# Output projection in two passes over tokens, with the FFN's input norm under the second pass

## The chip, the cores and the metric

The kernel runs as one program on the eight cores of one Trainium2 chip. Each core computes one half (1024 tokens) of one of four sequences; no core talks to another. The metric is the device time of the slowest core, in microseconds, median over executions. Some executions fall into a second, slower state, in which the cores of a die show a lower clock (in one execution of the changed kernel, of 2094.8 us, the mean granted clock was 0.808 to 0.809 on the four cores of one die and 0.982 to 0.985 on those of the other). The ratios leave those out and compare fast executions with fast ones; the medians are over all executions, and where slow ones are among them this is said.

Engines are named as the profile names them: PE is TensorE's matmul stream, PEld its weight loads, DVE is VectorE, ACT is ScalarE, POOL is GpSimd, which here only issues weight loads, and SP is SyncE.

## The reference, cut to what matters

```python
def rmsnorm(x, g):
    y = x * lax.rsqrt(jnp.mean(x * x, axis=-1, keepdims=True) + EPS)
    return y * g

x = x + hybrid_mixer(...)          # ends in  concat(y_conv, y_m) @ w_out
h = rmsnorm(x, norm_ffn_g)         # <- the norm of this study, D_MODEL = 2048
x = x + conv_ffn(h, ...)           # up = causal_dwconv3(h @ w_up) + b; (silu(g) * u) @ w_down
```

The output projection is a 2048 x 2048 product. The norm needs, for each token, the sum of squares over all 2048 features, so it can't start for a token before every output feature of that token has been projected.

## The kernel before

Activations lie feature-major: 16 tiles of 128 features, with 1029 tokens (1024 and a halo of 5) along the free dimension. Weights arrive as blocks of 256 output features (1 MB as bf16, converted by the load from 2 MB of float32) in four slots; a block's slot is refilled when its matmuls are done. One feature group is 48 matmuls: 16 contraction tiles times three token slices of about 343, into the three PSUM banks of psA or psB.

```python
def wout_task(b):                              # one weight block, two feature groups
    def consume(slot, Rs):
        for j in range(2):
            f = 2 * b + j
            ps, Rb = feat_major_proj(slot, Rs, j, yT, RyT, 16, wo_slices)
            P.op("dve", ...)                   # xres[:, f, 0:1029] += ps          (L841)
            sumsq_hook(f, 0, 1029, f == 0)     # ACT: tmpq = square (L445); DVE: acc += tmpq (L447)
    task(blk(w_out_b, b), 16, 256, consume)
for b in range(8):
    wout_task(b)

def norm_finish_sliced(col0, slices, goff, dst, Rdst2, Rrs_list):
    for si, (s0, w) in enumerate(slices):
        P.op("pe", ...)                        # psC = ones.T @ acc   (f32)       (L452)
        rstd_from_psum(...)                    # ACT: Ln, then Exp                (L381, L383)
        for k in range(16):
            P.op("dve", ...)                   # hT[:, k, slice] = xres * g * rstd (L456)

def conv_evac(ps, Rb, dst, Rdst, cidx):        # each group of the FFN's first product
    P.op("act", ...)                           # dst  = ps[:, :, 2:344] * w2 + b
    P.op("dve", ...)                           # dst += ps[:, :, 1:343] * w1
    P.op("dve", ...)                           # dst += ps[:, :, 0:342] * w0
# ... cut ...
```

The helper that records matmuls gives most of them one line, L508, so they are told apart by their tiles: `psA<-yT,wsl` with 343 columns is the output projection, `psA<-hT,wsl` with 344 columns the FFN.

## Time and profile before

| what | value | read from |
|---|---|---|
| median of the first six runs (one of them slow), lowest | 1794.5, 1792.4 us | times |
| PE busy | 94% of the span | page, part 1 |
| PE in the chain that ended last | 91% | page, part 4 |
| output projection | 561.7 to 674.1 us | chain of waits |
| first FFN group ends | 704.8 us | chain of waits |
| granted clock, 674.1 to 704.8 us | 0.69 | windows |

The page's part 1 (busy time, share of the span, instructions) and the first line of part 4, of the kernel before:

```profile
PE 1686.9 (94%) x11310; PEld 1073.3 (60%) x11310; DVE 725.0 (40%) x986; ACT 383.6 (21%) x535; POOL 67.3 (4%) x130
...
PE 91%; DVE 4%; ACT 2%; DMA 2%; issue 2%; DVEq 0%; SPq 0%; ACTq 0%
```

TensorE sets the time. To gain something one has to find where it waits. The timeline around the norm, slowest core (start, duration, engine, line, operation, tiles; in brackets the idle time before it and what ended it):

```profile
674.55 1.23 DVE L841 TENSOR_TENSOR arena<-psB,arena 128x1029 f32<-128x1029 f32 x1 [3.60 <-PE psB L508]
675.93 1.06 ACT L445 ACTIVATE regE<-arena 128x1029 f32<-128x1029 f32 x1 [6.31 <-DVE arena L841]
677.09 1.23 DVE L447 TENSOR_TENSOR regE<-regE 128x1029 f32<-128x1029 f32 x1 [1.31 <-ACT regE L445]
678.47 1.07 PE L452 MATMUL psC<-regE,cst_sb 128*128 128x345 f32 x2 [4.38 <-DVE regE L447]
...
680.78 23.45 DVE L456 SCALAR_TENSOR_TENSOR hT<-arena,cst_sb,regE 128x345 bf16<-128x345 f32 x48 [2.46 <-ACT regE L383]
...
692.72 12.10 PE L508 MATMUL psA<-hT,wsl 128*128 128x344 bf16 x25 [0.18 <-DVE hT L456]
```

The 48 multiplies of the norm take 23.45 us on DVE, and the first FFN group can only follow them. In the chain of waits (start, duration, what) the groups on either side of it show the normal pace, and the first full group after it is slower:

```profile
667.07 7.04 PE psB L508 x48
674.15 0.40 issue
...
683.23 7.47 DVE hT L456 x16
...
704.82 7.78 PE psB L508 x48
712.60 7.04 PE psA L508 x48
```

The windows view (stretch, length, busy time of PE, PEld, DVE, ACT, POOL, then granted clock, DMA share, GB/s written) shows the clock:

```profile
561.50:674.10 112.60, 112.59 (x770) 74.83 (x767) 36.20 (x30) 15.93 (x15) 4.23 (x8) 1.00 0.56 123
674.10:704.80 30.70, 21.57 (x55) 6.72 (x56) 25.91 (x50) 3.91 (x7) 0.53 (x1) 0.69 0.19 34
```

So the norm costs 704.8 - 674.1 - 7.04 = 23.6 us, and 0.7 us more in the slow group after it: 24.4 us. PE's "busy" 21.57 us in the gap are the ones-matmuls and then, for the most part, single matmuls one after the other, each waiting for a multiply.

### The profile page before, as it was taken

What the parts mean: (1) busy time and instruction counts of PE and PEld (TensorE: products, weight loads), DVE (VectorE), ACT (ScalarE), POOL (GpSimd) and SP (SyncE); (2) the same over time, 40 slices, a digit from 0 to 9 for tenths busy, and PEclk for the clock granted to TensorE, in tenths of its full rate; (3) what the DMA queues carried; (4) which work ended last, traced back from release to release, by engine and by line L of the source; (5) the groups of instructions that cost most, each with busy time, mean ns of one, the idle gap of its engine ahead of it and who ended that gap; (6) DMA issues with size and microseconds to landing.
All of it is one profiled execution on the core that took longest, in us unless ns stands there. A gap on an engine that the chain in (4) does not pass through costs nothing.

```text
span 1792.4 us, 27344 instructions; the slowest of 8 cores (1788.1 to 1792.4 us)
## 1 busy us (share of the span) xinstructions
PE 1686.9 (94%) x11310; PEld 1073.3 (60%) x11310; DVE 725.0 (40%) x986; ACT 383.6 (21%) x535; POOL 67.3 (4%) x130
## 2 busy tenths in 40 slices
PE   1999999999888997999999999999999999998995
PEld 1888868766665663666654466666445666543442
DVE  3543201234443336444441134444212444447556
ACT  3230022322331111222210022222000222212332
POOL 0000000000000000000000000000000000000000
PEclk9999999999999997999999999999999999998998
DMA  9944333333328531443344433444334443346774
GB/s 261 239 87 80 63 61 62 69 61 63 66 48 217 114 71 30 84 76 71 71 74 87 76 71 71 76 83 78 71 71 79 83 75 59 71 83 107 140 146 159
DMA packets 25577, 163.76 MB, mean 91 GB/s; under 512 B 3056, under 2 KB 3056, under 8 KB 8816
## 3 DMA queue, kind: packets, MB, share of 16 engines
q0 software_dynamic: 18400, 127.48, 39.7%
q1 hardware_dynamic: 7056, 34.55, 5.8%
q8 instruction: 91, 1.49, 0.3%
q14 instruction: 30, 0.25, 0.0%
HBM read 281.09 MB, written 8.39 MB: 162 GB/s over the span
## 4 chain that ended last, share of the span: by engine, by line
PE 91%; DVE 4%; ACT 2%; DMA 2%; issue 2%; DVEq 0%; SPq 0%; ACTq 0%
PE psB L508 38%; PE psA L508 30%; PE psB L494 9%; PE psA L967 5%; PE psA L494 4%; PE psB L967 2%; DMA arena<-xsl 2%; DVE hT L456 1%; DVE arena L996 1%; PE psC L403 0%; PE psB L971 0%; PE psA L680 0%; PE psC L542 0%; DVE regE L629 0%; ACT regE L652 0%
## 5 line engine op out<-in xcount | busy, mean ns | idle before, releaser
L508 PE MATMUL psB<-hT,wsl 128*128 128x344 bf16 (+2 forms) x3360 | 512.7, 314 | 7.2 <-DVE yT L729 7.2
L508 PEld LDWEIGHTS psB<-hT,wsl 128*128 128x128 bf16 x3360 | 330.6, 99 | 176.4 <-issue 7.8
L508 PE MATMUL psA<-hT,wsl 128*128 128x344 bf16 (+1 forms) x2208 | 345.2, 314 | 3.4 <-DVE hT L456 2.3
L508 PEld LDWEIGHTS psA<-hT,wsl 128*128 128x128 bf16 x2208 | 217.1, 98 | 124.8 <-issue 17.0
L508 PE MATMUL psA<-yT,wsl 128*128 128x512 bf16 (+1 forms) x1088 | 213.7, 354 | 0.8 <-DVE yT L891 0.8
L508 PE MATMUL psB<-yT,wsl 128*128 128x512 bf16 (+1 forms) x1088 | 213.4, 354 | 0.0
L508 PEld LDWEIGHTS psA<-yT,wsl 128*128 128x128 bf16 x1088 | 105.5, 97 | 103.3 <-issue 1.2
L508 PEld LDWEIGHTS psB<-yT,wsl 128*128 128x128 bf16 x1088 | 105.6, 97 | 102.6
L868 ACT ACTIVATE regE<-psA,cst_sb 128x1026 f32<-128x1026 f32 x44 | 53.1, 1207 | 406.3 <-PE psA L508 406.3
L494 PE MATMUL psB<-wsl,hT 128*128 128x256 bf16 x1152 | 128.6, 274 | 0.0
L870 DVE SCALAR_TENSOR_TENSOR regE<-psA,cst_sb,regE 128x1026 f32<-128x1026 f32 x44 | 56.6, 1286 | 170.8 <-ACT regE L868 170.8
L870 DVE SCALAR_TENSOR_TENSOR regE<-psB,cst_sb,regE 128x1026 f32<-128x1026 f32 x44 | 56.5, 1285 | 162.2 <-ACT regE L868 162.2
L494 PEld LDWEIGHTS psB<-wsl,hT 128*128 128x128 bf16 x1152 | 112.7, 98 | 13.5
L967 PE MATMUL psA<-hT,wsl 128*128 128x512 bf16 x352 | 88.3, 399 | 1.0
L868 ACT ACTIVATE regE<-psB,cst_sb 128x1026 f32<-128x1026 f32 x44 | 53.1, 1207 | 168.7 <-PE psB L508 168.7
L881 ACT ACTIVATE regE<-regE 128x1026 f32<-128x1026 f32 x44 | 46.6, 1059 | 123.5 <-DVE regE L872 123.5
L910 DVE TENSOR_TENSOR arena<-psB,arena 128x1024 f32<-128x1024 f32 x24 | 29.4, 1225 | 104.8 <-PE psB L508 104.8
L910 DVE TENSOR_TENSOR arena<-psA,arena 128x1024 f32<-128x1024 f32 x24 | 29.4, 1225 | 93.4 <-PE psA L508 93.4
L967 PEld LDWEIGHTS psA<-hT,wsl 128*128 128x128 bf16 x352 | 35.4, 101 | 52.1 <-issue 14.7
L445 ACT ACTIVATE regE<-arena 128x1029 f32<-128x1029 f32 (+1 forms) x30 | 31.8, 1060 | 151.6 <-DVE arena L841 89.7
L872 DVE SCALAR_TENSOR_TENSOR regE<-psA,cst_sb,regE 128x1026 f32<-128x1026 f32 x44 | 56.6, 1286 | 4.6
L872 DVE SCALAR_TENSOR_TENSOR regE<-psB,cst_sb,regE 128x1026 f32<-128x1026 f32 x44 | 56.5, 1285 | 4.6
(143 smaller groups left out, 1160.3 us busy)
## 6 DMA issues: line engine op xcount, KB each, us to landing
wsl<-w_up_b POOLq DMA_DIRECT2D x44, 1024.0 KB, 8.5
wsl<-w_in_b POOLq DMA_DIRECT2D x30, 1024.0 KB, 9.8
wsl<-w_down_b POOLq DMA_DIRECT2D x16, 1024.0 KB, 8.2
wsl<-w_pg_b POOLq DMA_DIRECT2D x16, 1024.0 KB, 8.6
arena<-xr SPq DMA_DIRECT2D x4, 2058.0 KB, 23.1
arena<-xsl SPq DMA_DIRECT2D x8, 1024.0 KB, 11.0
arena<-xsl SPq DMA_DIRECT2D x4, 2048.0 KB, 14.1
wsl<-w_out_b POOLq DMA_DIRECT2D x8, 1024.0 KB, 9.0
```

Of the source, the lines that this page charges most:

```text
L445: P.op("act", lambda e: e.activation(out=tmpq[:, 0:w], in_=xres[:, f, col0:col0 + w], func=AF.Square), reads=[Rxres[f]], writes=[Rtmpq])
L456: P.op("dve", lambda e, k=k, s0=s0, w=w: e.scalar_tensor_tensor(out=dst[:, k, s0:s0 + w], in0=xres[:, k, col0 + s0:col0 + s0 + w], scalar= ...
L494: P.op("pe", lambda e, k=k, t=t, ps=ps: e.matmul(ps[:, 0:ncol], lhsT=src[:, k, t * 128:(t + 1) * 128], rhs=slot[:, k, 0:ncol], start=(k == ...
L508: P.op("pe", lambda e, k=k, si=si, c0=c0, w=w: e.matmul(ps[:, si, 0:w], lhsT=slot[:, k, j * 128:(j + 1) * 128], rhs=src[:, k, c0:c0 + w], ...
L868: P.op("act", lambda e: e.activation(out=dst[:, :, :], in_=ps[:, :, 2:344], func=AF.Identity, bias=cs(C_FCB + cidx), scale=w2), reads=Rb + ...
L870: P.op("dve", lambda e: e.scalar_tensor_tensor(out=dst[:, :, :], in0=ps[:, :, 1:343], scalar=w1, in1=dst[:, :, :], op0=ALU.mult, op1=ALU.add),
L872: P.op("dve", lambda e: e.scalar_tensor_tensor(out=dst[:, :, :], in0=ps[:, :, 0:342], scalar=w0, in1=dst[:, :, :], op0=ALU.mult, op1=ALU.add),
L881: P.op("act", lambda e, j=j: e.activation(out=upg[j][:, :, :], in_=upg[j][:, :, :], func=AF.Silu), reads=[Rupg[j]], writes=[Rupg[j]])
L910: P.op("dve", lambda e, ps=ps, f=f: e.tensor_tensor(out=xres[:, f, 5:1029].rearrange("p (s n) -> p s n", s=2), in0=ps[:, 0:2, 0:512], in1= ...
L967: P.op("pe", lambda e, k=k, pg_=pg_, j=j: e.matmul(pg_[:, 0:512], lhsT=slot[:, k, j * 128:(j + 1) * 128], rhs=hT[:, k, 512 * s:512 * (s + ...
L996: P.op("dve", lambda e, k=k, xs=xs: e.scalar_tensor_tensor(out=xs, in0=xs, scalar=cs(C_GF + k), in1=rs2[:, 512 * s:512 * (s + 1)], op0=ALU ...
```

## The change

Its intent: tokens are cut into three slices. A first pass projects all 16 feature tiles for slices 0 and 1, after which these tokens are complete. A second pass projects slice 2, and under its matmuls run the statistics and the 32 multiplies of slices 0 and 1. The 16 multiplies of slice 2 run under the first two FFN groups, which are reordered to do slices 0 and 1 of both groups first. The four weight blocks that are still in the slots at the end of the first pass are used again at once; the other four are loaded a second time.

```diff
+    wo_at = [task(blk(w_out_b, b), 16, 256, wout_task(b, (0, 1), 0)) for b in range(8)]
+    call(norm2_begin)
+    for n, b in enumerate((4, 5, 6, 7)):
+        again(wo_at[b], wout_task(b, (2,), 8))            # slot still holds the block
+        if n == 0:
+            call(lambda: [norm2_stat(0), norm2_stat(1)])  # ones-matmul, Ln, Exp
+        call(lambda n=n: norm2_apply(n // 2, range(8 * (n % 2), 8 * (n % 2) + 8)))
+    for b in range(4):
+        task(blk(w_out_b, b), 16, 256, wout_task(b, (2,), 8))   # loaded again
...
     def ffg_task(jj):
         def consume(slot, Rs):
+            early = {}
+            if jj == 0:
+                for j in range(2):
+                    early[j] = next_group()
+                for sis in ((0, 1), (2,)):
+                    for j in range(2):
+                        for si in sis:
+                            if (si, j) == (1, 0):
+                                norm2_last_slice()        # ones-matmul and 16 multiplies of slice 2
+                            ...                           # 16 matmuls of this slice
             for j in range(2):
-                ps, Rb = feat_major_proj(slot, Rs, j, hT, RhT, 16, ff_slices, ff_src)
+                ps, Rb = early[j] if jj == 0 else feat_major_proj(...)
                 conv_evac(ps, Rb, upg[j], Rupg[j], c)
```

In the projection each slice now has its own PSUM bank, its own add, square and accumulation (343 columns instead of 1029). The token slices of the FFN moved by a few columns, so that the gated product is two DVE instructions instead of one. The other parts of the diff are bookkeeping of slots and aliases when the program is built.

More of the change, by code (lines that the diff above doesn't have):

```diff
@@ L338, in build_nc @@
     wstate = {"issued": 0}
-    def wget(i):
-        while wstate["issued"] < min(i + NS, len(wq)):
-            j = wstate["issued"]
-            src, kc, ncol = wq[j]
-            dst = wsl[:, j % NS, 0:kc * ncol].rearrange("p (k n) -> p k n", k=kc)
-            o = P.op("pool", lambda e, dst=dst, src=src: e.dma_start(out=dst, in_=src),
-                     writes=[Rslot[j % NS]], dma=True)
-            if j < NS and wstate.get("gate") is not None:
-                g = wstate["gate"]
-                g.signal = True
-                o.deps.append(g)
-            wstate["issued"] += 1
-        src, kc, ncol = wq[i]
-        return wsl[:, i % NS, 0:kc * ncol].rearrange("p (k n) -> p k n", k=kc), Rslot[i % NS]
     tasks = []
@@ L358, in task, with again @@
         tasks.append(("w", (src, kc, ncol), fn))
+        return len(tasks) - 1
+    def again(which, fn):
+        tasks.append(("h", which, fn))
     def call(fn):
@@ L363, in run_tasks, with issue @@
     def run_tasks():
-        for t in tasks:
+        load_of, last_use = {}, {}
+        for pos, t in enumerate(tasks):
             if t[0] == "w":
+                load_of[pos] = len(wq)
+                last_use[len(wq)] = pos
                 wq.append(t[1])
-        n = 0
-        for t in tasks:
-            if t[0] == "w":
-                slot, rs_ = wget(n)
-                n += 1
-                t[2](slot, rs_)
-            else:
-                t[2]()
+            elif t[0] == "h":
+                last_use[load_of[t[1]]] = pos
+        def issue(pos):
+            while wstate["issued"] < len(wq):
+                j = wstate["issued"]
+                if j >= NS and last_use[j - NS] >= pos:
+                    return
+                src, kc, ncol = wq[j]
+                dst = wsl[:, j % NS, 0:kc * ncol].rearrange("p (k n) -> p k n", k=kc)
+                o = P.op("pool", lambda e, dst=dst, src=src: e.dma_start(out=dst, in_=src),
+                         writes=[Rslot[j % NS]], dma=True)
+                if j < NS and wstate.get("gate") is not None:
+                    g = wstate["gate"]
+                    g.signal = True
+                    o.deps.append(g)
+                wstate["issued"] += 1
+        for pos, t in enumerate(tasks):
+            if t[0] == "c":
+                t[2]()
+                continue
+            issue(pos)
+            n = load_of[pos if t[0] == "w" else t[1]]
+            src, kc, ncol = wq[n]
+            t[2](wsl[:, n % NS, 0:kc * ncol].rearrange("p (k n) -> p k n", k=kc), Rslot[n % NS])
     def tap(name, ap, reads):
@@ L828, in build_nc @@
     call(xreload)
-    wo_slices = [(343 * s, 343) for s in range(3)]
-    n2_slices = [(0, 345), (345, 342), (687, 342)]
+    n2_slices = [(3, 343), (346, 342), (688, 341)]
     RhT2 = [[Res("hT2_%d_%d" % (k, si)) for si in range(3)] for k in range(16)]
@@ L833, in build_nc, with out_alias, wout_task @@
     Rrs2_3 = [Res("rs2_%d" % si) for si in range(3)]
-    ff_src = lambda k, si: [RhT2[k][si]] + ([RhT2[k][si - 1]] if si > 0 else [])
-    def wout_task(b):
+    ff_src = lambda k, si: [RhT2[k][1], RhT2[k][2 if si == 2 else 0]]
+    Rx1 = [[Res("x1_%d_%d" % (f, si)) for si in range(3)] for f in range(16)]
+    Racc3 = [Res("acc3_%d" % si) for si in range(3)]
+    wo_banks = {"i": 0}
+    sq_at = {"i": 0}
+    sq_late = []
+    def out_alias():
+        for f in range(16):
+            for si in range(3):
+                P.alias(Rx1[f][si], [Rxres[f]])
+        for si in range(3):
+            P.alias(Racc3[si], [Racc])
+            P.alias(Rrs2_3[si], [Rrs2])
+    call(out_alias)
+    def wout_task(b, sls, first_f):
         def consume(slot, Rs):
@@ L839, in consume @@
                 f = 2 * b + j
-                ps, Rb = feat_major_proj(slot, Rs, j, yT, RyT, 16, wo_slices)
-                P.op("dve", lambda e, ps=ps, f=f: e.tensor_tensor(out=xres[:, f, :].rearrange("p (s n) -> p s n", s=3),
-                                                                  in0=ps[:, :, 0:343], in1=xres[:, f, :].rearrange("p (s n) -> p s n", s=3),
-                                                                  op=ALU.add), reads=Rb + [Rxres[f]], writes=[Rxres[f]])
-                sumsq_hook(f, 0, 1029, f == 0)
@@ L845, in wout_task @@
-        task(blk(w_out_b, b), 16, 256, consume)
-    for b in range(8):
-        wout_task(b)
-    def norm2():
-        tap("x1", arena[:, 0:16464], Rxres)
+                for si in sls:
+                    c0, w = n2_slices[si]
+                    ps, Rb = (banksA + banksB)[wo_banks["i"] % 6]
+                    wo_banks["i"] += 1
+                    for k in range(16):
+                        P.op("pe", lambda e, k=k, ps=ps, c0=c0, w=w, j=j: e.matmul(
+                            ps[:, 0:w], lhsT=slot[:, k, j * 128:(j + 1) * 128], rhs=yT[:, k, c0:c0 + w],
+                            start=(k == 0), stop=(k == 15)), reads=[Rs, RyT[k]], writes=[Rb])
+                    xs = xres[:, f, c0:c0 + w]
+                    P.op("dve", lambda e, ps=ps, xs=xs, w=w: e.tensor_tensor(out=xs, in0=ps[:, 0:w], in1=xs, op=ALU.add),
+                         reads=[Rb, Rxres[f], Rx1[f][si]], writes=[Rx1[f][si]])
+                    a_ = acc[:, c0:c0 + w]
+                    qi = sq_at["i"] % 3
+                    q_ = tmpq[:, 343 * qi:343 * qi + w]
+                    if sq_late:
+                        sq_late.pop()()
+                    if f == first_f:
+                        P.op("act", lambda e, xs=xs, a_=a_: e.activation(out=a_, in_=xs, func=AF.Square),
+                             reads=[Rx1[f][si]], writes=[Racc3[si]])
+                    else:
+                        sq_at["i"] += 1
+                        P.op("act", lambda e, xs=xs, q_=q_: e.activation(out=q_, in_=xs, func=AF.Square),
+                             reads=[Rx1[f][si]], writes=[Rtmpq3[qi]])
+                        sq_late.append(lambda a_=a_, q_=q_, si=si, qi=qi: P.op(
+                            "dve", lambda e: e.tensor_tensor(out=a_, in0=a_, in1=q_, op=ALU.add),
+                            reads=[Racc3[si], Rtmpq3[qi]], writes=[Racc3[si]]))
@@ new lines, in wout_task, with norm2_stat @@
+        return consume
+    Rtmpq3 = [Res("tmpq3_%d" % si) for si in range(3)]
+    call(lambda: [P.alias(Rtmpq3[si], [Rtmpq]) for si in range(3)])
+    psDf = psD[:, :].bitcast(F32)
+    def norm2_stat(si):
+        while sq_late:
+            sq_late.pop()()
+        s0, w = n2_slices[si]
+        pst, Rpst = (psDf, RpsD) if si == 1 else (psC, RpsC)
+        P.op("pe", lambda e: e.matmul(pst[:, 0:w], lhsT=onesF, rhs=acc[:, s0:s0 + w], start=True, stop=True),
+             reads=[Racc3[si], Rcst], writes=[Rpst])
+        rstd_from_psum(pst[:, 0:w], rs2[:, s0:s0 + w], Rpst, Rrs2_3[si], 2048.0)
@@ L851, in norm2, with norm2_apply, norm2_begin @@
+    def norm2_apply(si, ks):
+        s0, w = n2_slices[si]
+        for k in ks:
+            P.op("dve", lambda e, k=k: e.scalar_tensor_tensor(
+                out=hT[:, k, s0:s0 + w], in0=xres[:, k, s0:s0 + w], scalar=cs(C_G2 + k), in1=rs2[:, s0:s0 + w],
+                op0=ALU.mult, op1=ALU.mult), reads=[Rx1[k][si], Rrs2_3[si], Rcst], writes=[RhT2[k][si]])
+    def norm2_begin():
         for k in range(16):
@@ L853, in norm2, with norm2_last_slice, norm2_end @@
                 P.alias(RhT2[k][si], [RhT[k]])
-        for si in range(3):
-            P.alias(Rrs2_3[si], [Rrs2])
-        norm_finish_sliced(0, n2_slices, C_G2, hT, RhT2, Rrs2_3)
+    wo_at = [task(blk(w_out_b, b), 16, 256, wout_task(b, (0, 1), 0)) for b in range(8)]
[7 more added lines that the diff above has]
+        task(blk(w_out_b, b), 16, 256, wout_task(b, (2,), 8))
+    def norm2_last_slice():
+        norm2_stat(2)
+        norm2_apply(2, range(16))
+    def norm2_end():
+        for f in range(16):
+            P.alias(Rxres[f], Rx1[f])
+        P.alias(Racc, Racc3)
+        P.alias(Rtmpq, Rtmpq3)
         for r in RaT:
@@ L860, in norm2 @@
             P.alias(r, conv_res + mlstm_small_res)
-    call(norm2)
-    ff_slices = [(1 + 342 * s, 344) for s in range(3)]
+    call(norm2_end)
+    ff_slices = [(3 + 341 * s, 344) for s in range(3)]
     groups = [(0, 16), (16, 16), (32, 12)]
@@ L876, in consume @@
         def consume(slot, Rs):
+            early = {}
[4 more added lines that the diff above has]
+                    for j in range(2):
+                        ps, Rb = early[j]
+                        for si in sis:
+                            if (si, j) == (1, 0):
+                                norm2_last_slice()
+                            c0, w = ff_slices[si]
+                            for k in range(16):
+                                P.op("pe", lambda e, k=k, ps=ps, si=si, c0=c0, w=w, j=j: e.matmul(
+                                    ps[:, si, 0:w], lhsT=slot[:, k, j * 128:(j + 1) * 128], rhs=hT[:, k, c0:c0 + w],
+                                    start=(k == 0), stop=(k == 15)), reads=[Rs] + ff_src(k, si), writes=[Rb[si]])
             for j in range(2):
                 c = 2 * jj + j
-                ps, Rb = feat_major_proj(slot, Rs, j, hT, RhT, 16, ff_slices, ff_src)
+                ps, Rb = early[j] if jj == 0 else feat_major_proj(slot, Rs, j, hT, RhT, 16, ff_slices, ff_src)
                 conv_evac(ps, Rb, upg[j], Rupg[j], c)
@@ L890, in consume @@
                 conv_evac(ps, Rb, upu[j], Rupu[j], 44 + c)
-                P.op("dve", lambda e, j=j, c=c: e.tensor_tensor(out=aT[:, c - g0, :].rearrange("p (s n) -> p s n", s=3),
-                                                                 in0=upg[j][:, :, :], in1=upu[j][:, :, :], op=ALU.mult),
+                P.op("dve", lambda e, j=j, c=c: e.tensor_tensor(out=aT[:, c - g0, 0:682].rearrange("p (s n) -> p s n", s=2),
+                                                                 in0=upg[j][:, 0:2, 0:341], in1=upu[j][:, 0:2, 0:341], op=ALU.mult),
+                     reads=[Rupg[j], Rupu[j]], writes=[RaT[c - g0]])
+                P.op("dve", lambda e, j=j, c=c: e.tensor_tensor(out=aT[:, c - g0, 682:1024], in0=upg[j][:, 2, :], in1=upu[j][:, 2, :], op=ALU.mult),
                      reads=[Rupg[j], Rupu[j]], writes=[RaT[c - g0]])
         task(blk(w_up_b, 22 + jj), 16, 256, consume)
-    wd_slices = [(2, 512), (514, 512)]
+    wd_slices = [(0, 512), (512, 512)]
     Rtl = Res("tbl")
```

## The prediction

> **What bounds the kernel.** TensorE. The page gives it 94% of the span busy and 91% of the chain that ended last; mean granted clock 0.978 (cores view). In the chain, each output-projection feature group (48 matmuls) takes 7.03 us, without a break from 561.7 to 674.1 us. DVE and ACT are hidden there.
>
> **What the change attacks.** The norm between output projection and FFN. The timeline shows, after the last projection matmul at 674.1: DVE add 1.24, ACT square 1.07, DVE add 1.24, ones-matmul 1.08, Ln and Exp 1.0, then 48 norm multiplies on DVE, 0.488 us apart, 23.45 us, ending 704.2. The first FFN group advances at that pace and ends at 704.8 instead of 674.1 + 7.0: 23.6 us lost. The granted clock in 674 to 705 is 0.69, and the next group takes 7.78 instead of 7.04: 0.7 more. Total about 24.4 us, all on the critical path: the ceiling (1.4%). [...]
>
> **Removed.** Two of three token slices are projected first (about 75 us); their statistics and 32 multiplies run under the third slice (37.5 us of matmuls), the last 16 multiplies under four FFN half-groups (9.4 us).
>
> **Added or moved** (estimates from trace durations)
> - TensorE: 3 columns fewer (-0.3 us). Three f32 ones-matmuls enter the stream, about 0.7 us each: +2.1.
> - DVE, second pass: per weight block two tiles at 1.04 us (two 343-column adds) plus 8 multiplies at 0.49, 6.0 us against 4.7 of TensorE, for four blocks. A lag of some 5 us; six PSUM banks hold 14, so no stall.
> - Last slice: ones-matmul after the first half-group, Ln/Exp, 16 multiplies: ready 12.2 us after the FFN starts; its matmuls want the last at 12.3. At most +0.3.
> - First FFN tile: both feature groups now end 2.35 us apart, while evacuating one takes 1.21 + 1.29 + 1.29, about 4.1 us. The third group waits for psA: +1.8 us, once.
> - DMA: 4 MB of projection weights are reloaded. A second-pass block lasts 4.7 us. In 30 to 38 us of this trace, when weight loads alone kept all 16 engines busy, they wrote 152 to 180 GB/s: about 6.3 us per block. [...] Five loads queued from 4.7 us on land at about 13.5, 20, 26, 32.5, 39; needed at 20, 25, 30, 34, 39. Just in time: stall 0 to 3 us, +0.5.
> - The gated product is two DVE instructions instead of one of 1.23 us: hidden except before w_down: +0.2.
>
> Sum: -24.4 + 4.6, about -20 us.
>
> **Prediction: 1775 us, 8 in 10 within 1770 to 1782.** Chances: faster by over 2% 0.01, within 2% 0.98, slower 0.01.
>
> **What would show it.** Windows: no TensorE idle over 0.5 us between projection and FFN except one wait of psA on the DVE convolution multiply of about 2 us; clock near 1.0 there. Tile view of hT: 32 multiplies under the projection, 16 under the first FFN tile. Waits: none or a short one of TensorE on a w_out DMA. FFN groups unchanged at 7.04 us.
>
> **What would make it wrong.** Weight loads slower than 6.3 us when all cores reload together (TensorE waiting on DMA, and a clock drop behind it); DVE lag reaching the PSUM banks; the third-slice chain being longer, so the first FFN tile still waits.

## The result, and the profile after

| | before | changed kernel |
|---|---|---|
| median | 1794.31 us (20 runs, four of them slow; the fast ones alone 1794.06) | 1776.80 us (10 runs) |
| range | 1792.43 to 1896.36 (slow runs in it) | 1775.78 to 1778.34 |
| ratio of fast runs | | 0.9905, 95% interval 0.9897 to 0.9914 |
| projection start to first w_down matmul, eight cores | 362.1 to 362.4 us | 343.0 to 346.2 us, median 344.6 |

A ratio is the mean time of one kernel's fast runs over that of the other's of the same rounds, so it is not quite the ratio of the medians quoted. The last row is the sharpest measure: on each core, the time from the start of the first projection matmul to the start of the first w_down matmul, read from the matmul records. It leaves out when a core reached the projection, which differs from core to core by up to 7 us. I call it *the stretch*. It comes from one profiled execution of each run: the changed kernel, profiled twice, gave medians of 344.6 and 346.0 us, so a difference of a microsecond between medians means little where loads or the clock are involved.

Part 1 of the page and the first line of part 4, changed kernel:

```profile
PE 1670.3 (94%) x11268; PEld 1072.5 (60%) x11310; DVE 737.2 (42%) x1092; ACT 389.7 (22%) x567; POOL 69.7 (4%) x134
...
PE 90%; DVE 4%; DMA 2%; issue 2%; ACT 2%; DVEq 0%; SPq 0%; ACTq 0%; POOLq 0%
```

The busy share of PE says nothing: it is 94% in both. The timeline of the norm's multiplies, L909 in the changed kernel, slowest core, shows them hidden: four batches of 8 under the second pass (slices 0 and 1), and 16 under the first FFN groups:

```profile
643.51 3.99 DVE L909 SCALAR_TENSOR_TENSOR hT<-arena,cst_sb,regE 128x343 bf16<-128x343 f32 x8 [0.41 <-ACT regE L393]
...
660.19 3.96 DVE L909 SCALAR_TENSOR_TENSOR hT<-arena,cst_sb,regE 128x342 bf16<-128x342 f32 x8
...
682.38 7.83 DVE L909 SCALAR_TENSOR_TENSOR hT<-arena,cst_sb,regE 128x341 bf16<-128x341 f32 x16 [3.86 <-ACT regE L393]
```

The chain of waits of that core, from the end of the first pass to the FFN's steady pace (L869 is the projection, L902 the ones-matmul, L968 the first FFN tile, L518 the later ones, L947 to L951 the evacuation of psA):

```profile
638.90 2.33 PE psB L869 x16
641.23 0.58 PE psC L902 x2
641.80 0.58 PE psD L902 x2
642.38 4.65 PE psB L869 x32
...
661.54 16.28 DMA wsl<-w_up_b
677.81 0.25 issue
678.06 2.51 PE psA L968 x16
680.57 0.57 PE psC L902 x2
681.14 2.33 PE psA L968 x16
683.48 4.68 PE psB L968 x32
688.15 2.20 PE psA L968 x15
...
690.76 1.22 ACT regE L947
...
692.07 1.30 DVE regE L949
...
693.46 1.30 DVE regE L951
...
695.09 8.86 PE psA L518 x48
703.95 7.03 PE psB L518 x48
```

The gap of 24.4 us is gone, but three new things stand in the chain. A weight load (the first FFN block) took 16.28 us from issue to landing, and TensorE waited for it. The third FFN group started only at 695.1, when psA had been evacuated. And that group took 8.86 us instead of 7.03. TensorE's waits in the same stretch, and the windows around them:

```profile
PE psA L518 <- DVE regE L951: 2.1, 1, 2.1
PE psA L968 <- DMA wsl<-w_up_b: 1.4, 1, 1.4
PE psB L869 <- DMA wsl<-w_out_b: 1.4, 1, 1.4
```

```profile
678.00:695.00 17.00, 14.95 (x98) 9.58 (x98) 10.92 (x19) 2.33 (x4) 0.53 (x1) 1.00 0.97 169
695.00:704.00 9.00, 8.91 (x50) 5.48 (x51) 2.57 (x2) 4.32 (x4) 0.00 (x0) 0.81 0.56 110
704.00:745.00 41.00, 41.00 (x282) 27.41 (x281) 20.98 (x20) 9.36 (x8) 1.59 (x3) 1.00 0.40 70
```

On the eight cores the psA wait is 2.0 to 2.1 us and the waits on weight loads add up to 1.9 to 3.2 us. On cores 3 and 7 the profile puts one of the latter down to a DVE instruction, but on all eight cores both waits end 0.24 to 0.25 us after the landing of the block, so they are the loads'. Cores 2 and 7 lose clock after the psA wait, cores 4 and 5 after the wait for the first FFN block, cores 0, 1, 3 and 6 never.

### The profile page after: what moved, and what is told of

Same layout as the page of the kernel before. It is cut to its first block, busy times and chain, and to the rows that moved or that the text cites. A ratio compares the mean times of both kernels' runs of the same rounds, so it can differ in the third digit from the quotient of the medians.

```text
span 1775.8 us, 27638 instructions; the slowest of 8 cores (1769.2 to 1775.8 us)
## 1 busy us (share of the span) xinstructions
PE 1670.3 (94%) x11268; PEld 1072.5 (60%) x11310; DVE 737.2 (42%) x1092; ACT 389.7 (22%) x567; POOL 69.7 (4%) x134
## 4 chain that ended last, share of the span: by engine, by line
PE 90%; DVE 4%; DMA 2%; issue 2%; ACT 2%; DVEq 0%; SPq 0%; ACTq 0%; POOLq 0%
PE psB L518 35%; PE psA L518 26%; PE psB L504 9%; PE psA L1063 4%; PE psA L504 4%; PE psA L869 3%; PE psB L869 3%; PE psB L1063 2%; DMA arena<-xsl 2%; DMA wsl<-w_up_b 1%; DVE arena L1092 1%; PE psC L413 0%; PE psB L1067 0%; DVE hT L466 0%; PE psA L690 0%
## 5 line engine op out<-in xcount | busy, mean ns | idle before, releaser
L518 PE MATMUL psB<-hT,wsl 128*128 128x344 bf16 (+2 forms) x3312 | 504.1, 313 | 7.2 <-DVE yT L739 7.2
L518 PEld LDWEIGHTS psB<-hT,wsl 128*128 128x128 bf16 x3312 | 325.6, 99 | 172.9 <-issue 7.8
L518 PE MATMUL psA<-hT,wsl 128*128 128x344 bf16 (+1 forms) x2160 | 328.4, 312 | 2.1 <-DVE regE L951 2.1
L518 PEld LDWEIGHTS psA<-hT,wsl 128*128 128x128 bf16 x2160 | 212.4, 98 | 111.2 <-issue 4.1
L518 PE MATMUL psA<-yT,wsl 128*128 128x512 bf16 x684 | 154.6, 378 | 2.1 <-DVE yT L988 1.0
L518 PE MATMUL psB<-yT,wsl 128*128 128x512 bf16 x694 | 155.3, 378 | 0.5
L947 ACT ACTIVATE regE<-psA,cst_sb 128x1026 f32<-128x1026 f32 x44 | 53.1, 1207 | 394.2 <-PE psA L518 385.8
L504 PEld LDWEIGHTS psB<-wsl,hT 128*128 128x128 bf16 x1152 | 112.7, 98 | 13.5
L518 PEld LDWEIGHTS psA<-yT,wsl 128*128 128x128 bf16 x704 | 68.1, 97 | 84.7 <-issue 1.5
L518 PEld LDWEIGHTS psB<-yT,wsl 128*128 128x128 bf16 x704 | 68.1, 97 | 83.9
L947 ACT ACTIVATE regE<-psB,cst_sb 128x1026 f32<-128x1026 f32 x44 | 53.1, 1206 | 166.8 <-PE psB L518 166.8
L1063 PEld LDWEIGHTS psA<-hT,wsl 128*128 128x128 bf16 x352 | 35.2, 100 | 52.0 <-issue 14.3
L869 PE MATMUL psB<-yT,wsl 128*128 128x342 bf16 (+2 forms) x384 | 57.5, 309 | 1.4 <-DMA wsl<-w_out_b 1.4
L951 DVE SCALAR_TENSOR_TENSOR regE<-psA,cst_sb,regE 128x1026 f32<-128x1026 f32 x44 | 56.6, 1286 | 4.6
L951 DVE SCALAR_TENSOR_TENSOR regE<-psB,cst_sb,regE 128x1026 f32<-128x1026 f32 x44 | 56.5, 1285 | 4.6
```

The lines of the kernel that those rows point to most:

```text
L504: P.op("pe", lambda e, k=k, t=t, ps=ps: e.matmul(ps[:, 0:ncol], lhsT=src[:, k, t * 128:(t + 1) * 128], rhs=slot[:, k, 0:ncol], start=(k == ...
L518: P.op("pe", lambda e, k=k, si=si, c0=c0, w=w: e.matmul(ps[:, si, 0:w], lhsT=slot[:, k, j * 128:(j + 1) * 128], rhs=src[:, k, c0:c0 + w], ...
L869: P.op("pe", lambda e, k=k, ps=ps, c0=c0, w=w, j=j: e.matmul(ps[:, 0:w], lhsT=slot[:, k, j * 128:(j + 1) * 128], rhs=yT[:, k, c0:c0 + w], ...
L947: P.op("act", lambda e: e.activation(out=dst[:, :, :], in_=ps[:, :, 2:344], func=AF.Identity, bias=cs(C_FCB + cidx), scale=w2), reads=Rb + ...
L951: P.op("dve", lambda e: e.scalar_tensor_tensor(out=dst[:, :, :], in0=ps[:, :, 0:342], scalar=w0, in1=dst[:, :, :], op0=ALU.mult, op1=ALU.add),
L1063: P.op("pe", lambda e, k=k, pg_=pg_, j=j: e.matmul(pg_[:, 0:512], lhsT=slot[:, k, j * 128:(j + 1) * 128], rhs=hT[:, k, 512 * s:512 * (s + ...
```

## The experiments

**My theory.** What the change left on the chain is (1) weight loads that come late, because a block is asked for every 4.65 us and served more slowly (on the slowest core the blocks landed 6.8 us apart on average); (2) the psA wait of 2.0 to 2.1 us; (3) a clock drop behind either (8.86 us for a group of 7.03). **Rivals.** A: DVE, which is asked for more than TensorE's time in the second pass (6.0 us against 4.7 per block, by the prediction's estimate from trace durations), holds the FFN's start. B: the waits stand in series, so that what one gives the next takes. C: most of the gain comes from the reordered first FFN tile and the narrower instructions, not from the second pass.

| run | result | median us | ratio to before, 95% interval | stretch on 8 cores: lowest, median, highest |
|---|---|---|---|---|
| changed kernel again | right | 1779.0 | 0.9900, 0.9885 to 0.9915 | 343.6, 346.0, 347.3 |
| no reload | wrong | 1776.8 | 0.9886, 0.9870 to 0.9903 | 342.5, 342.5, 342.7 |
| one full block | right | 1834.6 (two of four runs slow) | 0.9893, 0.9873 to 0.9913 | 341.9, 342.9, 343.5 |
| first tile evacuated by slice | right | 1776.9 | 0.9878, 0.9859 to 0.9898 | 341.5, 343.0, 344.0 |
| one full block and by slice | right | 1772.0 | 0.9877, 0.9863 to 0.9890 | 339.1, 340.3, 340.9 |
| two full blocks and by slice | right | 1770.8 | 0.9871, 0.9858 to 0.9885 | 339.9, 339.9, 340.1 |
| one pass | right | 1790.9 | 0.9978, 0.9964 to 0.9991 | 357.8, 359.3, 359.6 |
| two passes, norm late | right | 1790.2 | 0.9977, 0.9964 to 0.9991 | 356.8, 359.1, 361.1 |
| 12 filler matmuls | wrong on purpose | 1774.8, one run | one look | 342.6, 342.7, 342.8 |
| 24 filler matmuls | wrong on purpose | 1777.9, one run | one look | 346.0, 346.0, 346.2 |

The first four ran on a chip where before took 1796.7 us, the next four where it took 1794.3. The medians hold slow executions: one in rows 1, 2, 4 and 8, two in row 3. The fast ones alone have medians of 1778.8, 1776.0, 1777.5 (two runs), 1775.5 and 1790.2 us. The intervals of neighbouring rows overlap, since the effects are 0.1 to 0.4% of the time; the stretch and the waits are the same from core to core to a few tenths wherever no load is involved.

### The changed kernel again

> The changed kernel again, unaltered, so that the others of this call are compared with it on the same chip. All theories: 1776 to 1778 us; TensorE waits 2 to 3.5 us in all for the last projection block and the first FFN block to land, then 2.0 us for psA, and on some cores the granted clock drops after one of these waits.

Measured as expected in kind: 1779.0 us; on the slowest core the psA wait 2.0 us and 1.6 and 1.5 us on loads. Six of the eight cores lost clock once.

### No reload

```diff
-    for b in range(4):
-        task(blk(w_out_b, b), 16, 256, wout_task(b, (2,), 8))
+    for b in range(4):
+        again(wo_at[4 + b], wout_task(b, (2,), 8))       # wrong weights, no load
```

> Wrong result on purpose: the second pass uses the four resident blocks twice and loads none again. Theory (the reload is late by 2 to 3.5 us, because five 1 MB loads are asked for every 4.65 us and served every 6.3 us): the TensorE waits on weight loads vanish, about 1773.5 us, 3 us less than the changed kernel. Rival A (DVE's lag in the second pass is what holds the FFN's start; the DMA wait only comes last by chance): the wait stays but is now put down to DVE, time within 1 us of the changed kernel. Rival B (the waits are in series on one chain, so what one gives the next takes): the psA wait grows from 2.0 to about 5 us, time unchanged.

It came out as my theory said for the waits. The only wait of TensorE left between projection and FFN on the slowest core is

```profile
PE psA L518 <- DVE regE L951: 2.0, 1, 2.0
```

The waits on loads vanish on all eight cores, so they were the loads' own: rival A fell, since DVE did the same work and held nobody, and rival B fell in its first form, since the psA wait stayed at 2.0. The stretch fell by 3.5 us at the median (346.0 to 342.5). But it did not fall by what the waits on loads were worth on every core: cores that had kept their clock (343.6 and 343.8 us in the changed kernel) gained only 0.9 and 1.3 us. All eight cores now lost clock after the psA wait. I had expected 1773.5 us and got 1776.8 (1776.0 in fast runs), which led to the filler runs below.

### One full block

```diff
-    wo_at = [task(..., wout_task(b, (0, 1), 0)) for b in range(8)]
+    wo_at = [task(..., wout_task(b, (0, 1, 2) if b in (4,) else (0, 1), ff0)) for b in range(8)]
-    for n, b in enumerate((4, 5, 6, 7)):
+    # second pass: blocks 5, 6, 7 again, then 0, 1, 2, 3 loaded; multiplies after the first four of them
```

> Block 4 does all three slices in the first pass, so its slot is free for a reload 28 us earlier and only three blocks are held. Right result. Theory: the first reload is out of the queue before the second pass starts, the others have 4.65 us more slack; waits on weight loads at most 0.7 us, about 1774 us. Rival A (DVE lag): the second pass is one block (4.7 us) shorter and covers less of DVE's work, so the wait of TensorE on DVE before the third slice's statistics grows by 2 to 4 us and the time is 1777 or more. Rival B: psA wait grows, time unchanged.

The waits for the projection's own blocks shrank to at most 0.7 us, but the first FFN block still came late on six cores, by up to 2.3 us in the waits, where I had allowed 0.7. On three cores the profile puts a wait at one of these places down to a DVE instruction and not to the load. The landing times settle it for the FFN's start: on every core that waited there, the first FFN matmul starts 0.24 to 0.25 us after the block has landed. The stretch fell to 342.9. No wait of the third slice's ones-matmul on DVE appeared, so rival A's mechanism did not show; the time on the clock, 1776.7 and 1778.3 us in the two fast runs, missed the expected 1774 and by itself would have suited rival A. Two cores without any wait on a load lost clock after the psA wait; the six others kept it.

### First tile evacuated by slice

```diff
-                conv_evac(ps, Rb, upg[j], Rupg[j], c)
+                if jj == 0 and j == 0:
+                    for si in range(3):
+                        conv_evac(ps, Rb, upg[j], Rsl[si], c, si)    # 342 columns, one bank each
+                else:
+                    conv_evac(ps, Rb, upg[j], Rupg[j], c)
```

> The first FFN feature group is evacuated slice by slice (three times three instructions of 342 columns), so each psA bank comes free by itself. Theory: the wait of the third feature group on psA (2.0 us) vanishes, since its first bank is free 1.4 us after the last norm multiply, before the second group ends; 2.0 us less, and on the cores that lost clock after that wait about 2 us more: 1773 to 1774.5 us. The waits on weight loads stay. Rival B (waits in series): the next group waits instead, on psB, by the same amount; time unchanged.

The psA wait is gone and nothing took its place: the group after it waits 0.2 us for psB. TensorE's waits on the slowest core:

```profile
PE psA L971 <- DMA wsl<-w_up_b: 1.7, 1, 1.7
PE psB L869 <- DMA wsl<-w_out_b: 1.5, 1, 1.5
PE psA L869 <- DVE regE L888: 0.3, 1, 0.3
PE psB L518 <- DVE regE L954: 0.2, 1, 0.2
```

No core lost clock in the stretch, though waits on loads of up to 2.5 us stayed. The stretch fell by 3.0 us at the median, to 343.0. Rival B fell for good. The time on the clock was 1776.9 us against 1779.0 beside it (1775.5 against 1778.8 in fast runs), where I had expected 1773 to 1774.5 on a chip that proved 2 us slower than the first.

### Both remedies

```diff
+    wo_at: blocks (4,) or (4, 5) do slices 0, 1 and 2 in the first pass
+    conv_evac of the first FFN group slice by slice
```

> As both2, but only block 4 does all three slices early and three blocks are held. Theory: waits on weight loads of 0 to 2.5 us stay on some cores (as in the run with one full block), no wait of the third slice's ones-matmul on DVE, psA wait gone; 339 to 341.5 us for the stretch, 1772 us, ratio about 0.987.

> Blocks 4 and 5 do all three slices in the first pass (two slots free early, two blocks held), and the first FFN feature group is evacuated slice by slice. Right result. Theory (weight loads, psA wait and the clock drop behind a wait of over 2 us are the three terms): no TensorE wait on a weight load, no psA wait, clock 1.00 on all cores from projection to w_down; from the first projection matmul to the first w_down matmul 339 us (before 362, changed kernel 343 to 347), 1771 us, ratio to before about 0.986. The shorter cover (six blocks instead of eight) leaves DVE behind by 3.3 us at the end of the second pass, so the ones-matmul of the third slice, which stands 2.35 us into the FFN, may wait about 1 us. Rival A (DVE lag decides): that wait is 3 us or more and the stretch is 342 or longer.

With one full block: 340.3 us at the median; three cores without any wait on a load take 339.1, the others wait 0.9 to 1.4 us for the first FFN block. With two full blocks all eight cores take 339.9 to 340.1, the clock is 1.00 throughout, and what is left on the slowest core is

```profile
PE psC L902 <- DVE regE L888: 0.6, 1, 0.6
PE psB L518 <- DVE regE L958: 0.2, 1, 0.2
```

The first line is the ones-matmul of slice 2 waiting for DVE, which is behind because the shorter second pass covers less: the one place where rival A's DVE lag shows, 0.6 us where about 1 was expected. **Two full blocks with the evacuation by slice take 1770.8 us: 23.5 us less than before (ratio 0.9871; the changed kernel had 0.9905 and 0.9900 in its rounds).** The result is right, and the median is the lowest, though its interval overlaps that of one full block with the evacuation by slice.

### One pass

```diff
-    (both passes)
+    for b in range(8):
+        task(blk(w_out_b, b), 16, 256, wout_task(b, (0, 1, 2), ff0))
+    call(lambda: [norm2_stat(0), norm2_stat(1), norm2_apply(0, range(16)), norm2_apply(1, range(16))])
```

> The projection in one pass over all three slices, as before; only the first FFN tile keeps the new order (slices 0 and 1 of both feature groups, then slice 2) and the narrow tail. No reload. Theory (what pays is the cover of the second pass): TensorE still waits about 20 us for statistics and 32 multiplies; the two first FFN groups end some 32 to 33 us after the last projection matmul instead of 38.4, and 2 us go to psA: a gain of 4 us over before, stretch 358 us, 1790 us. Rival C (the reordering of the first FFN tile and the narrower instructions give most of the gain, the second pass little): 1782 us or less.

1790.9 us, 3.4 less than before, as expected from the cover theory and far from rival C's 1782. TensorE waits for the multiplies (8.8 us in one piece, then matmul by matmul):

```profile
PE psA L964 <- DVE hT L909: 8.8, 1, 8.8
PE psA L518 <- DVE regE L947: 2.0, 1, 2.0
PE psD L902 <- DVE regE L888: 0.6, 1, 0.6
```

The reordered first tile and the narrower instructions together give about 3 us of stretch (362.1 to 359.3); with both in place, the second pass gives the other 15 (359.3 to 344.6). No run separates the reordering from the narrower instructions, and none has the covering second pass with the old order of the first tile.

### Two passes, norm late

```diff
+    (both passes, without norm2_apply between)
+    for si in range(3):
+        norm2_stat(si); norm2_apply(si, range(16))
     # first FFN tile in the old order
```

> The projection in two passes with the reload, but the whole norm after it and the first FFN tile in the old order. Theory (two passes alone gain nothing and cost the late reload): one wait of 0.5 to 2 us on the last projection block, the tail before the ones-matmul shorter by 2.4 us because its three instructions are a third as wide, the 48 multiplies in the open as before: stretch 361 to 362.5 us, within 2 us of before. Rival C: 1788 us or less.

1790.2 us, 4 us less than before, with a stretch of 359.1 us at the median where I expected 361 to 362.5, and still above the 1788 of rival C. It has the reload's cost (on the slowest core 3.3 us of waits on projection blocks) and no cover. What it gains is the tail. The first multiply starts 2.5 us after the last projection matmul on all eight cores, where it was 6.6 to 7.0 us before (my reading of the records), since add, square and accumulation run over 341 columns instead of 1029 and the first ones-matmul no longer waits for them; the last of the three waits 1.0 us. So the shorter tail is worth some 4 us without any cover, and the reload's waits take 0.7 to 3.3 us of it back. The run with one pass has the same 2.5 us, so the tail alone could account for its 3 us.

### Filler matmuls

The run without reload left a riddle: the same wait for psA halved the clock on all eight cores there, on two in the changed kernel (two more lost it after the longer wait for the first FFN block), on two with one full block. I count idling as the time from the start of one matmul to the start of the next, less the 0.147 us at which they normally follow each other (48 in 7.03 us). So counted the wait is 2.15 us; the profile, which lets the last matmul end 0.31 us after its start, shows 2.0. The clock records of the trace come in steps of 3.413 us, so I laid the waits over that grid. In the run without reload the wait began between 0.07 us before and 0.24 us after a grid point on all eight cores, so that 2.08 us of it or more fell into one window. On the cores that kept their clock in the changed kernel and with one full block it lay across a grid point (in the changed kernel with at most 1.55 us of it in one window). To test it, the wait was moved along the grid:

```diff
     again(wo_at[b], wout_task(b, (2,), 8))
+    if n == 2:                    # 12, or 24, matmuls of 344 columns into psC, read by nobody
+        call(filler)
```

> The run without reload (wrong result on purpose) plus 12 matmuls of 344 columns that nobody reads, after the third block of the second pass: 1.76 us more TensorE work, and the 2.15 us psA wait comes 1.76 us later. Theory (the clock is granted by fixed windows of 3.41 us, and is halved for the next window when about 2.1 us of idling falls inside one; in the run without reload the wait began within 0.3 us of a window's start on all cores): the wait now straddles two windows, the clock stays 1.00 on all eight cores, and from the first projection matmul to the first w_down matmul it takes 342.5 us as without the filler: 1.76 more work, 1.7 less lost clock. Rival (any wait of 2.15 us halves the clock for a while, and cores that kept it in other runs did so by chance): the clock drops on most cores, 344.3 us.

> As the run with 12 filler matmuls, with 24 of them: 3.51 us, one window and 0.1 us. Theory: the wait falls wholly inside one window again, the clock drops on all eight cores, 346 us from the first projection matmul to the first w_down matmul. If the filler itself keeps the clock up by doing work shortly before the wait, the clock stays as with 12: 344.3 us.

Both came out as the window theory said, on eight of eight cores each: 12 fillers, the clock stays at 1.00 and the stretch is 342.6 to 342.8 us, as without them; 24 fillers, the clock drops on every core, 346.0 to 346.2 us. TensorE's wait, then the windows after it on core 2, with 12 fillers:

```profile
PE psA L518 <- DVE regE L957: 2.0, 1, 2.0
```

```profile
690.00:693.00 3.00, 1.82 (x13) 1.26 (x14) 0.93 (x1) 1.98 (x2) 0.26 (x1) 1.00 0.40 57
693.00:695.00 2.00, 2.00 (x16) 1.32 (x15) 0.44 (x1) 1.46 (x2) 0.00 (x0) 1.00 1.17 188
```

and with 24:

```profile
693.00:695.00 2.00, 0.72 (x5) 0.26 (x3) 1.90 (x2) 0.00 (x0) 0.53 (x1) 1.00 0.11 21
695.00:697.00 2.00, 1.29 (x8) 0.86 (x9) 0.46 (x1) 1.45 (x2) 0.00 (x0) 0.91 0.38 41
697.00:699.00 2.00, 2.00 (x9) 1.03 (x7) 0.00 (x0) 1.98 (x2) 0.00 (x0) 0.50 0.81 115
```

The wait is the same 2.0 us. In one case 2 us hold 16 matmuls right after it, in the other 9. So 1.76 us of useless work cost nothing, because they moved a wait across a window's edge.

This explains why the cores of the changed kernel differ. The loads' waits, which vary from core to core (1.9 to 3.2 us in sum), shift the later psA wait along the grid, and only some cores have it inside one window. It also explains why taking the loads' waits away gained less than they measured. In all twelve kept traces the projection starts 1.7 to 2.2 us after a grid point on every core. Part of the reason can be read from the trace of before, though no run tests it: the 48 matmuls just ahead of the projection start inside a half-clock window on seven of the eight cores, and the later they start in it, the less of them is slowed. On core 4, which starts 0.01 us into the window, the projection begins 8.71 us later; on core 6, which starts 0.62 us into it, 8.41 us later. So the window halved what one of these cores was ahead of the other on the grid.

## Why the prediction was right, point by point

The measured median, 1776.8 us, is 1.8 us above the predicted 1775 and inside the range 1770 to 1782; "within 2%" was given 0.98.

| step of the prediction | predicted | measured, slowest core of the changed kernel |
|---|---|---|
| gap removed (48 multiplies, tail, slow group) | -24.4 us | gone; multiplies at 643.5 to 664.2 and 682.4 to 690.2 |
| columns dropped | -0.3 | groups of 7.00 to 7.01 for 7.03, 16 times: about -0.4 |
| three ones-matmuls in the stream | +2.1 | 0.58 + 0.58 + 0.57 = +1.7 |
| last slice's multiplies late | at most +0.3 | about 0: the third slice's matmuls keep pace until the last |
| third group waits for psA | +1.8 | +2.1 |
| weight loads just in time | +0.5 (0 to 3) | 1.4 + 1.4 = +2.8 |
| gated product in two | +0.2 | w_down's wait for it 1.0 instead of 0.8: +0.2 |
| clock drop behind a wait | only named as a risk | 8.86 for 7.03: +1.8, on four of eight cores |

The measured terms after the first add up to 8.2 us, against 4.6 predicted. 362.1 - 24.4 + 8.2 = 345.9 us is what this core's stretch should be; it was 346.1. So the table leaves out no more than 0.2 us. The sum was off by 3.6 us on this core, twice what the median was off: that the median came within 1.8 us is in part luck, since the rest lies in when the cores reach the projection, which I did not study.

**The gap.** Right in kind and size, and the runs without cover (one pass and norm late, with stretches of 359.3 and 359.1 us) show that cover is what removes most of it. A float32 add of two tensors took 1.23 us over 1029 columns in the kernel before and 0.51 to 0.52 us over 341 to 343 in the changed kernel, so splitting an instruction in three costs DVE about 0.3 us, which is hidden, and shortens a tail that is not.

**The DVE lag.** Right: DVE fell behind (on the slowest core the add of a group started up to 5.4 us after the group's last matmul, by my reading of the records, where some 5 us were predicted) and no PSUM bank ran out: from the second pass to the first FFN matmul of the changed kernel the two waits of TensorE, 1.9 to 3.2 us in sum, ended with the landing of a block. The lag only shows with two full blocks, where the second pass is a quarter shorter, at 0.6 us.

**The loads.** Right in mechanism, too small in the sum: 2.8 us where 0.5 was entered. The service time was nearly right: on the slowest core the five queued blocks landed 14.1, 21.1, 28.8, 35.0 and 41.2 us after the end of the first pass, against 13.5, 20, 26, 32.5 and 39, so 6.8 us apart on average instead of 6.3. With needs 4.65 us apart, half a microsecond per block is all it takes. The prediction named a range of 0 to 3 us for the stall and then entered 0.5, the low end, although its own numbers left no margin for the last block. From 650 to 690 us the changed kernel's DMA engines were fully busy (share 1.01 in the windows) and wrote 164 GB/s, inside the 152 to 180 GB/s from which the prediction took its 6.3 us per block; the float32 sources are twice the size, so by my estimate they read 328 GB/s.

**The clock.** The step that was not in the sum. I took the expected wait of 2 us for safe; no trace had shown that. The trace I predicted from already spoke against it: just ahead of the projection a wait of 2.5 us stands on all eight cores of the kernel before, each with a half-clock window of 3.41 us behind it, and on the slowest core the group there takes 8.69 us, where 7.03 to 7.09 is normal. The filler runs show that 2.15 us is enough if it falls inside one window. A half-clock window cost 1.7 to 1.8 us on four of the eight cores, on two behind the psA wait and on two behind a load, and since the slowest core counts, it is in the time.

**What stays open.** The stretch explains 16 to 19 us per core and the median fell by 17.5; the time at which each core reaches the projection differs by up to 7 us, before and after, and I did not study it. Nor is it shown why one window with 2.11 us of idling left the clock alone.

## What to carry to other kernels

When work is moved under a matmul stream, list every new short wait on that stream, and price each twice: once for its length, and once for the half-clock window that can come behind it (here a wait of 2.15 us inside one window brought a window of 3.41 us at half clock, which cost 1.7 to 1.8 us); a finer release of buffers, one PSUM bank at a time, removed both here. The second pass over the weights asked for loads faster than the first did, every 4.65 us instead of every 9.33; compare the pace of demand with the measured pace of service, and let a few blocks finish early so that their slots are refilled ahead of time (with two full blocks no wait on a load was left). And test cover and reordering apart: here the reordering with the narrower instructions gave 3 us and the cover 15.

## The clock and the loads, as measured here

- Waits of some 2 us between matmuls were not safe here. A wait of 2.15 us halved the clock for the next 3.41 us on 8 of 8 cores when it lay inside one window (24 fillers), and on none of 8 when it lay across two (12 fillers). Laid over the trace's clock records, single waits with 2.06 us or more of idling in one window halved the clock in the twelve kept traces, but for one of 2.11 (in the changed kernel 2.24, 2.54, 2.38 and 2.15 us on cores 2, 4, 5 and 7); those with up to 2.04 us did not (windows that hold several waits are not counted here).
- In the fast executions profiled here, with eight cores running random data, the mean granted clock was 0.977 to 0.980 before and 0.982 to 0.986 after, and 1.00 through the projection of the kernel before; the clock records of all twelve kept traces hold only the shares 1.0 and 0.5, and 0.81 appears there only as the mean of a stretch. In the slow state it is otherwise: one execution of the changed kernel (2094.8 us) had a mean of 0.808 to 0.809 on all four cores of one die. Slow executions were not profiled, so which shares make up that mean is not shown.
- 1 MB blocks of bf16 loaded from 2 MB of float32, on all cores at once, landed 6.2 to 7.7 us apart on the slowest core, at 164 GB/s written, which is by my estimate 328 GB/s read.
